# Which queue parks and fetches turned slabs, and where a short convolution stands in a projection, in a two-layer hybrid encoder

## The chip, the cores and the metric

One Trainium2 chip; the kernel uses one core. The metric is the device time of one execution in microseconds (us). Engines are named as in the profile: PE (TensorE), DVE (VectorE), ACT (ScalarE), POOL (GpSimd) and SP (SyncE, which only issues DMAs).

## The reference

Two layers of one block on x of 512 positions by 2048, with 256 memory tokens. Cut to what matters:

```python
for l in range(DEPTH):                       # DEPTH = 2
    h = rmsnorm(x, pre_norm_g[l])
    z = h @ w_in[l]                          # 2048 -> 4928 columns
    q_lat, kv_lat, k_pe, gb, gc, xin, q_mem, gate = split_cols(z)
    q = rmsnorm(q_lat, q_norm_g[l]) @ w_uq[l]            # 8 heads of 128 + 64, rotary on the 64
    kv = rmsnorm(kv_lat, kv_norm_g[l]) @ w_ukv[l]
    a_out = mla_attention(q, k, v)                       # k_pe, rotated, is shared by the heads
    u = gc * xin
    c_out = gb * conv3(u, conv_w[l])                     # width 3 over positions, 512 channels
    m_out = memory_attention(q_mem, rmsnorm(mem), w_mk[l], w_mv[l])
    y = concat([a_out, c_out, m_out]) * silu(gate)
    x = x + rmsnorm(y @ w_o[l], post_norm_g[l])
```

All is float32. The kernel makes each float32 product of three matmuls of a high and a low half.

## The kernel before

**Products.** The projection and the output projection use a Strassen-like scheme with seven products P1 to P7 in place of eight. The left operands (sums of quarters of h, each split in a high and a low half) lie in 14 slabs for the whole of a layer's projection: seven operands of two slabs each. A slab is a tile of 128 x 2048 float32; there are `SLABS = 19` of them (line 61), shared by everything that is large. The columns of `w_in` are taken in five groups: 0 (gc and xin), 1 (gb and part of the gate), 2 (the latents `lat` and the rotary key), 3 (part of the gate, gm, and the memory queries, qm), 4 (the rest of the gate, ga0 and ga1). Groups 2 to 4 use the passes `STEADY` (line 493): P1, then P5 and P2 in turn, then P6 and P3 in turn, then P7, then P4. Each product has four steps, one per block of weights, so a group has 28 steps: P1 is steps 0 to 3, P5/P2 4 to 11, P6/P3 12 to 19, P7 20 to 23, P4 24 to 27. A step is 12 matmuls.

**Weights.** A block of 128 x 1024 (512 KB) is loaded by SP into one of 8 `raw` buffers (line 157 through line 146). Some blocks are summed in place on DVE (L178: P5 and P6 add their block to that of P1). ACT casts the block to the high half `wh` (L189), DVE subtracts it to get the low half `wl` (L190); there are three buffers of each. P4 and P7 turn a block already there into another one by a DMA that adds (`more`, line 163, issued by POOL as soon as the `wl` that reads the old values is made): eight in a group, four for P4 and four for P7. In P6/P3 all eight `raw` buffers hold blocks that P7 and P4 still use.

**Passes end** in `ended` (line 551): the product's PSUM banks are read by ACT or DVE into the slabs of the group. P6, P7 and P4 go on adding into the banks of P1. In group 3 the end of P6 is the first write into the slab of qm; the matmuls of P7 that follow use the same banks.

**Parked slabs.** A result of the projection has positions on partitions; the mixer wants channels there. DVE transposes 32 x 32 blocks in place (L767, L1031, L1032), `sent` (line 938) writes the slab to DRAM by one DMA per part (L945), and `fetched` (line 948) reads it back into a slab in another order by four DMAs (L952). gb, gc, the latents ql and kvl (kvl in two parts), qm, gm, ga0 and ga1 go this way: 9 writes and 32 fetches in a layer. All of them are issued by SP, between its weight loads. After a fetch, `latents_parts` and `qm_parts` split the latents and qm in halves, and `conv` works.

**Convolution.** `conv_back` (line 967) fetches u (from gc) and y (from gb). `conv(l, c)` (line 971) does a quarter of the channels: two operations on ACT (L974, the copy that reads u, and L975), three on DVE (L976, L977, L979), in small tiles of which there are four. Its u slab is free when the fourth quarter has copied it.

**Order.** The source lists the steps of a group with other work between them (`put`, `add`; lines 1604 to 1661). For a step the program also prepares the blocks of the next two steps and issues loads up to eight blocks ahead. One line decides which engines keep that order:

```python
with tc.manual_schedule(engines={mybir.EngineType.PE, mybir.EngineType.SP, mybir.EngineType.Pool}):
    pr.run()
```

(line 1709). DVE and ACT are ordered when the kernel is built. Every engine, SP and POOL included, works through its own list in order, so an entry that waits holds up those behind it. The tile framework also decides at that time which free slab a new tile takes.

Other traffic that POOL issues in these stages: the memory keys and values (`mem_fetch`, L918), the rotary table (L1068), and in the mixer the rotated queries, written in two DMAs (L1107) and read back as QR in four (L1112) for each half of the heads.

Of the kernel before, what the change touches and what calls it, by code (L numbers as in the profile page):

```python
# [85 lines left out]
class Program:  # L86
# [23 lines left out]
    def add(self, fn, units=(), room=0.0, ahead=None):  # L110

        self.steps.append((list(units), fn, room, self.ahead if ahead is None else ahead))
# [115 lines left out]
def encoder(tc, x, xt, mem, memt, positions, columns, w_in, q_norm_g, w_uq, w_qr, kv_norm_g, w_ukv,  # L228
# [3 lines left out]
    nc = tc.nc  # L232
# [16 lines left out]
    add = pr.add  # L249

    G = {}
    n_id = [0]

    def nm(s):
        n_id[0] += 1
        return f"{s}_{n_id[0]}"
# [4 lines left out]
    def slab(name, dt=F32):  # L261
        return slabs.tile([P, D], dt, tag="slab", name=nm(name))

    def scrap(name, w=512, dt=F32):
        return piece.tile([P, 512], dt, tag="piece", name=nm(name))[:, :w]
# [657 lines left out]
    def spots(t, c=4):  # L923

        return t.rearrange("q (p c k) -> q c p k", p=4, c=c)

    def by_tokens(a):
        return a.rearrange("q (p k) -> q p k", p=4)
# [9 lines left out]
    def sent(key, *parts):  # L938

        n = sum(t.shape[-1] for t in parts) // 4  # L940
        d = G["sent", key] = dram.tile([4, P, n], F32, name=nm(f"sent{key}"))
        o = 0
        for t in parts:
            w = t.shape[-1] // 4
            nc.sync.dma_start(d[:, :, o:o + w].rearrange("b q k -> q b k"), t.rearrange("q (b k) -> q b k", b=4))  # L945
            o += w

    def fetched(key, name, c=4):

        t, d = slab(name), G.pop(("sent", key))  # L950
        for b in range(4):
            nc.sync.dma_start(t[32 * b:32 * b + 32, :512 * c].rearrange("i (p k) -> i p k", p=4),  # L952
                              d[b].rearrange("(p i) k -> i p k", p=4))
        return t

    def sent_rows(name, C):
        def f():
            pr.until(lambda: C.get((name, "turned")) == NT)
            sent(name, C[name, "slab"])
        return f  # L960

    def gate_back(k, name):
        def f():
            G["ys"][k] = spots(fetched(name, "y"))
        return f

    def conv_back():
        G["uw"] = fetched("gc", "u")
        G["ys"][2] = spots(fetched("gb", "y"))

    def conv(l, c):
        def f():
            u, y, w, g = scrap("u"), scrap("conv"), G[f"cw{l}"], G["ys"][2][:, c]
            nc.scalar.copy(by_tokens(u), spots(G["uw"])[:, c])  # L974
            nc.scalar.activation(y, u, AF.Copy, scale=w[:, 1, c:c + 1])  # L975
            nc.vector.scalar_tensor_tensor(y[:, 1:], u[:, :S - 1], w[:, 0, c:c + 1], y[:, 1:], op0=ALU.mult, op1=ALU.add)  # L976
            nc.vector.scalar_tensor_tensor(y[:, :S - 1], u[:, 1:], w[:, 2, c:c + 1], y[:, :S - 1],  # L977
                                           op0=ALU.mult, op1=ALU.add)
            nc.vector.tensor_tensor(g, by_tokens(y), g, op=ALU.mult)  # L979
        return f  # L980
# [32 lines left out]
    def latents_begin(l, C):  # L1013
        q, kv = G["ql"], G["kvl"] = slab("ql"), slab("kvl")
        tiles_of = lambda a: a.rearrange("p (g t j) -> p t g j", t=NT, j=32)
        normalise([v[:, :QR_] for v in C["lat"]], QR_, G["grow"][0], tiles_of(q), SC_MLA)
        normalise([v[:, O_KV:O_KV + KVR] for v in C["lat"]], KVR, G["grow"][1], tiles_of(kv[:, :1024]))

    def k_rope(l, C):
        m = scrap("kpm").rearrange("p (b t s i) -> p b t s i", b=2, t=NT, s=2)  # L1020
        m1, m2 = m[:, 0], m[:, 1]
        for t in range(NT):
            kp = C["lat"][t][:, O_PE:O_PE + ROPE].rearrange("p (s i) -> p s i", s=2)
            nc.vector.tensor_tensor(m1[:, t], kp, G["cos2"][:, t], op=ALU.mult)
            for s in range(2):
                nc.vector.tensor_tensor(m2[:, t, s, :], kp[:, 1 - s, :], G["sin2"][:, t, s, :], op=ALU.mult)
        kr = G["kvl"][:, 1024:1536].rearrange("p (g t j) -> p t g j", t=NT, j=32)
        nc.vector.tensor_tensor(kr[:, :, :2], m1, m2, op=ALU.add)
        nc.scalar.copy(kr[:, :, 2:], kr[:, :, :2])
        for h in (slice(0, 1024), slice(1024, D)):  # L1030
            pr.defer(1.2, lambda h=h: nc.vector.transpose(G["ql"][:, h], G["ql"][:, h]))  # L1031
        pr.defer(1.8, lambda: nc.vector.transpose(G["kvl"][:, :1536], G["kvl"][:, :1536]))  # L1032
        pr.defer(0.0, lambda: G.update(normalised=l))

    def latents_sent(l):
        pr.until(lambda: G.get("normalised") == l)
        sent("ql", G.pop("ql"))
        kv = G.pop("kvl")
        sent("kvl", kv[:, :1024], kv[:, 1024:1536])
# [429 lines left out]
    def put(*passes):  # L1469
        for steps in passes:  # L1470
            for s in steps:
                add(*s)
# [20 lines left out]
    for l in range(depth):  # L1493
        G["left"] = L = Left(l > 0)
        C, gs, owns = projection(l)
# [44 lines left out]
        else:  # L1540
            put(ms[:1])
            add(use)
            for n in range(8):
                t, h = n // 2, n % 2
# [60 lines left out]
        steps = [s for passes in gs[2] for s in passes]  # L1605
# [9 lines left out]
        steps = [s for passes in gs[3] for s in passes]  # L1615
        put(steps[:2])
        add(lambda l=l, C=C: latents_begin(l, C))
        put(steps[2:5])
        add(conv_back)
        put(steps[5:8])  # L1620
        add(lambda l=l, C=C: k_rope(l, C))
        put(steps[8:18])
        add(lambda l=l: pr.until(lambda: G.get("normalised") == l))
        put(steps[18:20])
        add(conv(l, 0))
        put(steps[20:22])
        add(conv(l, 1))
        put(steps[22:23])
        add(lambda l=l: latents_sent(l))
        put(steps[23:24])  # L1630
        add(conv(l, 2))
        put(steps[24:26])
        add(conv(l, 3))
        put(steps[26:])
        add(owns[4])
        g4 = [s for steps in gs[4] for s in steps]
        put(g4[:3])
        add(latents_back)
        put(g4[3:6])
        add(sent_rows("qm", C))  # L1640
        if l == 0:
            add(tables_wide)
        put(g4[6:8])
        add(sent_rows("gm", C))
        put(g4[8:9])
        add(latents_parts)
        put(g4[9:11])
        add(lambda: G.update(qmw=fetched("qm", "QmL")))
        put(g4[11:14])
        if l == 0:  # L1650
            add(tables_turned)
        put(g4[14:20])
        add(qm_parts)
        put(g4[20:23])
        add(gate_back(3, "gm"))
# [97 lines left out]
```

## Time and profile before

| | |
|---|---|
| median of 3 runs | 1486.68 us (1485.53 to 1490.99) |
| the profiled execution | 1484.13 us, span 1482.3 us |
| granted TensorE clock, mean | 0.987 |
| PE busy | 98% of the span |
| DVE, ACT, POOL busy | 77%, 59%, 16% |
| DMA | 309.60 MB, 209 GB/s in the mean |
| weight loads of w_in by SP, 512 KB each | median 5.8 us to landing |

A line of a group of instructions reads: source line, engine, operation, the tile written and the tiles read, shape, count, then busy time and mean nanoseconds of one, then idle time of the engine just before them and what ended it. A line of waits reads: who waited, for whom, total us, times, longest. In a timeline the columns are start, duration (us), engine, line, operation; brackets hold the idle time before it. SPq and POOLq stand for a queue's DMA issues. In the time before, groups 3 and 4 of the first layer lie between about 271 and 435 us, of the second between about 1006 and 1170 us.

### The profile page before, as it was taken

The numbers are of one execution on the slowest core, as the hardware profiler recorded it, in microseconds if no ns is written. First come the engines' busy times: TensorE is split into PE (matmuls) and PEld (weight loads), VectorE is DVE, ScalarE is ACT, GpSimd is POOL, SyncE is SP. The second block draws the span as 40 slices with busy tenths as digits, with TensorE's granted clock in tenths as the row PEclk, the third lists the DMA queues.
The fourth block names the chain that finished last, engine by engine and source line by source line (L and its number), as shares of the span: only waits on it lengthen the run. The fifth ranks groups of instructions, "written<-read, shape, count | busy, mean of one in ns | idle before, by whom it ended". The sixth has DMA issues, their size and how long they took to land.

```text
span 1482.3 us, 19184 instructions
## 1 busy us (share of the span) xinstructions
PE 1445.9 (98%) x6944; PEld 1227.9 (83%) x6944; DVE 1140.0 (77%) x1517; ACT 869.6 (59%) x1330; POOL 239.7 (16%) x248
## 2 busy tenths in 40 slices
PE   9999999989899999999999999999898999999997
PEld 8888889868788888888898888998687888888886
DVE  5899688877667778868879666768766777688687
ACT  7856344644557788654777434445444586776543
POOL 0031302120111010321210333021201110003101
PEclk9999999989999999999999999999899999999999
DMA  9999959688899293795987999596888993228983
GB/s 358 404 271 212 222 157 234 177 174 251 214 276 253 69 270 93 134 224 155 336 288 226 239 229 218 186 209 169 174 249 208 292 242 90 53 86 147 258 177 128
DMA packets 155039, 309.60 MB, mean 209 GB/s; under 512 B 11009, under 2 KB 35073, under 8 KB 151105
## 3 DMA queue, kind: packets, MB, share of 16 engines
q1 hardware_dynamic: 105472, 194.86, 42.8%
q0 software_dynamic: 49472, 113.52, 37.1%
q8 instruction: 54, 0.88, 0.3%
q14 instruction: 41, 0.33, 0.1%
HBM read 270.47 MB, written 37.88 MB: 208 GB/s over the span
## 4 chain that ended last, share of the span: by engine, by line
PE 75%; issue 9%; DVE 6%; DMA 5%; POOL 2%; ACT 2%; POOLq 0%; SPq 0%; DVEq 0%; ACTq 0%
PE P L273 17%; PE P L274 17%; PE P L272 17%; DMA wr<-in_w_in_dram 3%; PE ptp L1219 2%; DVE wl L190 2%; POOL wr L146 2%; PE o L273 1%; PE o L274 1%; PE o L272 1%; PE sc L274 1%; PE sc L273 1%; PE sc L272 1%; PE sc L1200 1%; PE qps L274 1%
## 5 line engine op out<-in xcount | busy, mean ns | idle before, releaser
L189 ACT CAST wh<-wr 128x1024 fp32r<-128x1024 f32 (+2 forms) x436 | 443.6, 1023 | 442.3 <-PE P L274 311.1
L190 DVE TENSOR_TENSOR wl<-wr,wh 128x1024 fp32r<-128x1024 f32 (+2 forms) x436 | 513.6, 1184 | 219.9 <-ACT wh L189 216.9
L272 PE MATMUL P<-wh,S 128*128 128x512 f32 (+1 forms) x896 | 346.6, 387 | 12.5 <-ACT wh L189 12.5
L273 PE MATMUL P<-wl,S 128*128 128x512 f32 (+1 forms) x896 | 346.7, 387 | 3.7 <-DVE wl L190 3.7
L274 PE MATMUL P<-wh,S 128*128 128x512 f32 (+1 forms) x896 | 345.3, 385 | 0.0
L272 PE MATMUL P<-wh,A 128*128 128x512 f32 (+1 forms) x656 | 254.5, 388 | 6.2 <-ACT wh L189 6.2
L273 PE MATMUL P<-wl,A 128*128 128x512 f32 (+1 forms) x656 | 254.1, 387 | 2.4 <-DVE wl L190 2.4
L274 PE MATMUL P<-wh,A 128*128 128x512 f32 (+1 forms) x656 | 253.3, 386 | 0.0
L146 POOL DMA_DIRECT2D wr<-in_w_in_dram x108 | 130.3, 1212 | 503.3 <-DVE wl L190 399.5
L272 PEld LDWEIGHTS P<-wh,S 128*128 128x128 f32 x896 | 169.8, 189 | 44.1 <-ACT wh L189 13.3
L273 PEld LDWEIGHTS P<-wl,S 128*128 128x128 f32 x896 | 169.5, 189 | 36.5 <-DVE wl L190 6.0
L274 PEld LDWEIGHTS P<-wh,S 128*128 128x128 f32 x896 | 169.6, 189 | 30.5
L272 PEld LDWEIGHTS P<-wh,A 128*128 128x128 f32 x656 | 124.1, 189 | 29.2 <-ACT wh L189 7.0
L273 PEld LDWEIGHTS P<-wl,A 128*128 128x128 f32 x656 | 124.2, 189 | 26.3 <-DVE wl L190 4.4
L274 PEld LDWEIGHTS P<-wh,A 128*128 128x128 f32 x656 | 124.3, 189 | 22.4
L146 POOL DMA_DIRECT2D wr<-in_w_o_dram x40 | 48.5, 1286 | 299.0 <-DVE wl L190 293.3
L1206 ACT ACTIVATE P<-sc,nm 128x512 f32<-128x512 f32 (+1 forms) x96 | 59.7, 622 | 27.1 <-DVE nm L1203 26.9
L178 DVE TENSOR_TENSOR wr<-wr,wr 128x1024 f32<-128x1024 f32 (+1 forms) x60 | 69.6, 1164 | 7.1 <-DMA wr<-in_w_in_dram 6.5
L1209 ACT ACTIVATE P<-P,rec 128x512 f32<-128x512 f32 (+1 forms) x96 | 62.4, 661 | 7.5 <-DVE rec L1208 7.5
L1203 DVE TENSOR_REDUCE nm<-sc 128x1 f32<-128x512 f32 (+1 forms) x96 | 56.7, 594 | 10.4 <-PE sc L1201 9.3
L1219 PE MATMUL ptp<-identr,P 128*128 128x128 f32 x320 | 46.1, 272 | 0.3 <-ACT P L1209 0.3
L1219 PEld LDWEIGHTS ptp<-identr,P 128*128 128x128 f32 x320 | 38.2, 140 | 6.5 <-ACT P L1209 0.7
(311 smaller groups left out, 2053.4 us busy)
## 6 DMA issues: line engine op xcount, KB each, us to landing
wr<-in_w_in_dram SPq DMA_DIRECT2D x128, 512.0 KB, 5.8
wr<-in_w_in_dram POOLq DMA_DIRECT2D x92, 512.0 KB, 7.8
wr<-in_w_o_dram SPq DMA_DIRECT2D x48, 512.0 KB, 6.3
wr<-in_w_o_dram POOLq DMA_DIRECT2D x40, 512.0 KB, 6.7
wr<-in_w_in_dram SPq DMA_DIRECT2D x32, 416.0 KB, 4.1
wr<-in_w_mk_dram SPq DMA_DIRECT2D x15, 512.0 KB, 8.6
wr<-in_w_mv_dram SPq DMA_DIRECT2D x15, 512.0 KB, 9.9
wr<-in_w_in_dram POOLq DMA_DIRECT2D x16, 416.0 KB, 6.6
```

Source lines behind the costliest of these rows:

```text
L146: engine.dma_start(dst, src, **kw)
L178: nc.vector.tensor_tensor(tiles[a], tiles[a], tiles[b], op=ALU.add)
L189: pin(nc.scalar.copy(hi[:, h], src[:, h]))
L190: pin(nc.vector.tensor_tensor(lo[:, h], src[:, h], hi[:, h].bitcast(F32), op=ALU.subtract))
L272: nc.tensor.matmul(ps, ah, bh, start=first, stop=False, **kw)
L273: nc.tensor.matmul(ps, ah, bl, start=False, stop=False, **kw)
L274: nc.tensor.matmul(ps, al, bh, start=False, stop=last, **kw)
L1200: nc.tensor.matmul(by_tokens(ps), q, G["KA"], start=False, stop=False)
L1203: nc.vector.tensor_reduce(nmax, ps, axis=AX.X, op=ALU.max, negate=True)
L1206: nc.scalar.activation(pt, ps, AF.Exp, bias=nmax, accum_out=tot)
L1209: nc.scalar.activation(pt, pt, AF.Copy, scale=rec)
L1219: nc.tensor.transpose(ps[:, k * P:(k + 1) * P], pt[:, k * P:(k + 1) * P], G["ident"])
```

## The change

The DMAs of `sent` and `fetched` are issued by GpSimd instead of SyncE. In group 3, the fetch of u and y moves from behind step 4 to behind step 2; the four quarters of the convolution move from behind steps 19, 21, 23 and 25 of group 3 to behind steps 21 and 24 of group 3 and steps 0 and 2 of group 4; the write of the latents moves from behind step 22 to behind step 20. In group 4, the fetch of the latents moves from behind step 2 to behind step 1, the writes of qm and gm from behind steps 5 and 7 to behind steps 4 and 5, the latents' split from behind step 8 to behind step 6, and the fetch of qm from behind step 10 to behind step 9. In the first layer the rotary table's transposes move from behind step 13 to behind step 8. Steps are counted from 0 here.

```diff
         for t in parts:
             w = t.shape[-1] // 4
-            nc.sync.dma_start(d[:, :, o:o + w].rearrange("b q k -> q b k"), t.rearrange("q (b k) -> q b k", b=4))
+            nc.gpsimd.dma_start(d[:, :, o:o + w].rearrange("b q k -> q b k"), t.rearrange("q (b k) -> q b k", b=4))
             o += w
...
         for b in range(4):
-            nc.sync.dma_start(t[32 * b:32 * b + 32, :512 * c].rearrange("i (p k) -> i p k", p=4),
+            nc.gpsimd.dma_start(t[32 * b:32 * b + 32, :512 * c].rearrange("i (p k) -> i p k", p=4),
                               d[b].rearrange("(p i) k -> i p k", p=4))
...
-        put(steps[2:5])
+        put(steps[2:3])
         add(conv_back)
-        put(steps[5:8])
+        put(steps[3:8])
         add(lambda l=l, C=C: k_rope(l, C))
         put(steps[8:18])
         add(lambda l=l: pr.until(lambda: G.get("normalised") == l))
-        put(steps[18:20])
+        put(steps[18:21])
+        add(lambda l=l: latents_sent(l))
+        put(steps[21:22])
         add(conv(l, 0))
-        put(steps[20:22])
+        put(steps[22:25])
         add(conv(l, 1))
-        put(steps[22:23])
-        add(lambda l=l: latents_sent(l))
-        put(steps[23:24])
-        add(conv(l, 2))
-        put(steps[24:26])
-        add(conv(l, 3))
-        put(steps[26:])
+        put(steps[25:])
         add(owns[4])
         g4 = [s for steps in gs[4] for s in steps]
-        put(g4[:3])
+        put(g4[:1])
+        add(conv(l, 2))
+        put(g4[1:2])
         add(latents_back)
-        put(g4[3:6])
+        put(g4[2:3])
+        add(conv(l, 3))
+        put(g4[3:5])
         add(sent_rows("qm", C))
+        put(g4[5:6])
+        add(sent_rows("gm", C))
         if l == 0:
             add(tables_wide)
-        put(g4[6:8])
-        add(sent_rows("gm", C))
-        put(g4[8:9])
+        put(g4[6:7])
         add(latents_parts)
-        put(g4[9:11])
-        add(lambda: G.update(qmw=fetched("qm", "QmL")))
-        put(g4[11:14])
+        put(g4[7:9])
         if l == 0:
             add(tables_turned)
-        put(g4[14:20])
+        put(g4[9:10])
+        add(lambda: G.update(qmw=fetched("qm", "QmL")))
+        put(g4[10:20])
         add(qm_parts)
```

## The prediction, made before the result was known

> **What bounds the kernel now.** I read the page first, then who TensorE (PE) waits for, then the stretches in which it waits, and last the queues of the engines that release it.
>
> ```profile
> PE 1445.9 (98%) x6944; PEld 1227.9 (83%) x6944; DVE 1140.0 (77%) x1517; ACT 869.6 (59%) x1330; POOL 239.7 (16%) x248
> ```
>
> ```profile
> PE P L272 <- ACT wh L189: 18.6, 4, 6.2
> PE P L273 <- DVE wl L190: 6.1, 9, 1.0
> ```
>
> PE is the bound: whatever does not open or close a gap in PE costs nothing. Of its waits four carry nearly all, each for a weight block's high half `wh` (18.6 us), then for the low half `wl` of the same block. By window they lie in groups 3 and 4 of the projection, one in each, in both layers:
>
> ```profile
> 309.40:322.30 12.90, 5.66 (x13) 3.99 (x13) 12.10 (x15) 5.00 (x6) 3.66 (x3) 0.60 0.40 66
> 387.60:397.20 9.60, 5.78 (x14) 4.06 (x13) 6.30 (x7) 5.61 (x7) 0.00 (x0) 0.65 0.39 98
> 1045.20:1059.50 14.30, 7.05 (x17) 5.01 (x16) 12.13 (x14) 5.89 (x7) 3.67 (x3) 0.64 0.44 73
> 1124.10:1134.55 10.45, 6.39 (x16) 4.62 (x15) 7.15 (x8) 5.62 (x7) 0.82 (x1) 0.67 0.44 105
> ```
>
> Columns: stretch, length, then busy time and (instructions) of PE, weight load, DVE, ACT, POOL, granted clock, DMA share, GB/s. I set the edges where even pace ends and returns. The pace is in PE's timeline, at the start of group 3 and at the first gap:
>
> ```profile
> 270.71 0.39 PE L272 MATMUL P<-wh,A 128*128 128x512 f32 x1
> ...
> 271.39 0.39 PE L272 MATMUL P<-wh,A 128*128 128x512 f32 x1
> ```
>
> ```profile
> 309.20 0.39 PE L274 MATMUL P<-wh,S 128*128 128x512 f32 x1
> 315.83 0.79 PE L272 MATMUL P<-wh,S 128*128 128x512 f32 x1 [6.24 <-ACT wh L189]
> ```
>
> Three matmuls in 0.68 us is one each 0.227 us, a step of 12 in 2.72 us, a group of 28 steps in 76.2 us; 309.20 ends step 13 (counted from 0), and step 14 waits. The windows hold 12, 12, 15 and 14 matmuls of their own (the x counts less one or two tails from before the edge), worth 2.7, 2.7, 3.4 and 3.2 us. So the gaps cost 12.9-2.7 = 10.2, 9.6-2.7 = 6.9, 14.3-3.4 = 10.9 and 10.45-3.2 = 7.3 us: **35.3 us** in all. That is more than the 24.7 us of waiting, because the granted clock is only 0.60 to 0.67 there.
>
> Why does the first gap come? DVE and ACT:
>
> ```profile
> 310.16 0.75 DVE L976 SCALAR_TENSOR_TENSOR conv<-u,cols,conv 128x511 f32<-128x511 f32 x1 [0.85 <-ACT conv L975]
> ...
> 313.42 1.22 DVE L178 TENSOR_TENSOR wr<-wr,wr 128x1024 f32<-128x1024 f32 x1
> ...
> 321.56 0.42 DVE L386 COPY widecos<-cos 128x512 f32<-128x512 f32 x1
> ```
>
> ```profile
> 386.52 0.59 ACT L578 COPY ga<-P 128x512 f32<-128x512 f32 x1 [5.62 <-PE P L274]
> 387.88 0.58 ACT L578 COPY ga<-P 128x512 f32<-128x512 f32 x1 [0.77 <-PE P L274]
> 388.36 1.05 ACT L277 CAST ckv<-ckvL 128x1024 fp32r<-128x1024 f32 x1
> 389.31 0.62 ACT L277 CAST ckvL<-ckvL 128x512 fp32r<-128x512 f32 x1
> 389.83 1.04 ACT L189 CAST wh<-wr 128x1024 fp32r<-128x1024 f32 x1
> ```
>
> The sum that step 14 needs (L178 at 313.42) stands in DVE's queue behind conv work whose source lines come six to twelve steps later; even `tables_wide` (L386, from group 4) ran at 321.56. So DVE and ACT do not follow the source: line 1709 fixes only PE, SP and POOL, and the build orders DVE and ACT by when it believes inputs arrive. The second gap is order alone: ACT idles 5.62 us, copies a finished pass out, splits `ckv`, and only then (389.83) casts the block PE wants. Why would the build believe weights are late? SP's queue:
>
> ```profile
> 289.74 1.89 SPq L952 DMA_DIRECT2D u<-sentgc  x4
> 291.68 3.01 SPq L952 DMA_DIRECT2D y<-sentgb  x4
> 295.71 0.39 SPq L146 DMA_DIRECT2D wr<-in_w_in_dram  x1
> ```
>
> ```profile
> 368.09 1.47 SPq L146 DMA_DIRECT2D wr<-in_w_in_dram  x2
> ```
>
> ```profile
> DMA to landing us min/median/max: 9.5/9.7/10.2
> ```
>
> ```profile
> DMA to landing us min/median/max: 8.2/8.3/8.5
> ```
>
> ```profile
> wr<-in_w_in_dram SPq DMA_DIRECT2D x128, 512.0 KB, 5.8
> ```
>
> Right ahead of both gaps eight slab fetches stand in front of weight loads, and those (three issued 295 to 300, two 368 to 370) take 9.7 and 8.3 us to land against a median of 5.8. The pair of 368.09 had landed by 377.7, long before 389.83: in the second gap the data were there and only the order was wrong.
>
> **The change part by part.** *SP loses 9 writes and 32 fetches a layer.* Its weight loads no longer queue behind slabs, in the chip or in the build's timeline. I therefore let the build put sums and casts ahead of conv and latent splits, and take the 35.3 us off. The bounds are 0 (order unchanged) and 35.3; I stand near the upper end, since all four gaps follow the same eight fetches and no other stretch with a weight stream has such a gap.
>
> The Trainium skill (DMA: Bandwidth & Descriptors, SWDGE vs HWDGE vs iDMA) says each DMA engine takes turns between hardware and software queues. By that rule weights would share the engines with the moved slabs rather than stand behind them; no row here has slabs on POOL beside weights on SP, and the sum does not use it.
>
> *POOL gains them.*
>
> ```profile
> L1112 POOL DMA_DIRECT2D QR<-qrd x16 | 8.8, 555 | 11.1 <-PE sc L274 4.9 <-DMA qrd<-qrh 3.5 <-DMA qrd<-rm 2.1
> L146 POOL DMA_DIRECT2D wr<-in_w_in_dram x108 | 130.3, 1212 | 503.3 <-DVE wl L190 399.5 <-DMA wr<-in_w_in_dram 68.0 <-issue 21.5
> ```
>
> ```profile
> DMA to landing us min/median/max: 5.9/10.0/13.5
> ```
>
> ```profile
> sentql<-ql SPq DMA_DIRECT2D x2, 1024.0 KB, 6.3
> ```
>
> ```profile
> 301.51 1.27 POOL L146 DMA_DIRECT2D wr<-in_w_in_dram  x1 [23.06 <-DVE wl L190]
> ```
>
> The third row is QR's. A slab fetch has its size and costs POOL 0.56 us. For a write (twice the rows of a 1.2 us weight accumulate) I bound 0.56 to 2.4 and take 1.2, nearest in kind. Per layer 32 x 0.56 + 9 x 1.2 = 29 us (23 to 40): POOL goes from 240 to about 298 us, 20% busy, nothing on the path. Landing, 10.0 us for that size, stays under the lead of the fetches. What is queued behind them on POOL: the fetch of u and y, behind step 2 of group 3, stands after the two `pow` of the latents and ahead of eight weight accumulates (L146), the first at 301.5; even if it leaves as late as SP's did (289.7), it is issued by 294.2, 7 us before. The latents' writes stand behind all eight. The qm fetch, now behind step 9 of group 4, stands ahead of that group's accumulates; the first of these is used at step 20, ten steps or 27 us later. I cost all of this at 0, hidden under those 7 and 27 us; with that cover gone PE waits in P7 or P4, microsecond for microsecond. In the mixer the ga writes now precede the QR traffic on POOL:
>
> ```profile
> PE sc L1200 <- DMA QR<-qrd: 0.2, 1, 0.2
> ```
>
> QR has no spare time in one layer. The writes leave earlier than from SP, and the ga fetches then follow QR instead of running beside it; I cost 0, with up to 2.4 x 2 = 5 us a layer lost or 0.2 gained.
>
> The Trainium skill (SBUF — State Buffer, Who interferes with whom) speaks against the change: GpSimd cannot write descriptors while DVE runs in a two-port mode, so such DMAs belong on SP. If every DVE operation here counted, each of the 41 issues a layer could wait for one of about 1.2 us, 49 us more of POOL and still off the path; the 1212 ns above, with DVE 77% busy, show no such stretch for this mix.
>
> *Conv.*
>
> ```profile
> L976 DVE SCALAR_TENSOR_TENSOR conv<-u,cols,conv 128x511 f32<-128x511 f32 x4 | 3.0, 740 | 0.8 <-ACT conv L975 0.8
> L977 DVE SCALAR_TENSOR_TENSOR conv<-u,cols,conv 128x511 f32<-128x511 f32 x4 | 3.0, 738 | 0.1
> L979 DVE TENSOR_TENSOR y<-conv,y 128x512 f32<-128x512 f32 x4 | 2.6, 685 | 0.0
> ```
>
> 8.6 us of DVE in group 3; two quarters move on, 4.3 us, if the build follows (it hoists freely, so perhaps not). DVE stays crowded there, and I leave 2 us a layer of small PE waits (0 to 4.3). Group 4 gets as much and has idle DVE time in the 6.9 us gap: 0.
>
> The sum: -35.3 + 2 x 2 = -31.3 us. The profiled execution took 1484.1 (span 1482.3 and 1.8 around it), so 1452.8; it lies 2.6 us under the median of the runs, 1486.7, and the forecast for the median is **1455.4**. With the QR and DVE bounds this case reaches from 1451 to 1470.
>
> **The rivals.** *A slab comes free too late.* In group 3 fourteen of the 19 slabs hold left operands; gm, ql, kvl, u and y fill the rest. Before, conv's last copy of u ran in the first gap, ahead of that eviction, and qm could take u's place. Now conv 2 and 3 stand in group 4, and unless the build hoists their copies, qm's first eviction waits until ql is written out, behind POOL's last accumulate:
>
> ```profile
> 330.81 1.20 POOL L146 DMA_DIRECT2D wr<-in_w_in_dram  x1 [1.51 <-DVE wl L190]
> ```
>
> That is 8.5 us after step 15 began (322.3); plus 1.2, plus 6.3 landing, qm is evicted 16.0 us after it, while P7 needs the bank after 5 steps, 13.6 us. PE waits 2.4 us plus two evictions of 0.7 (the size of L979's), and at 2.4 us per write and slower landing up to 8, with the clock loss: about 7 a layer, 1455.4 + 14 = **1469**. Against it: ACT is idle enough to copy u early.
>
> *The order stays.* The build may still see late weights, or hoist conv because its data come earlier. Then gaps move but remain: **1487**, within 7. For it: conv was hoisted up to twelve steps.
>
> *ACT and DVE wait for POOL's slabs (slower).* If the build believes fetches land sooner than they do, a split or conv copy stands at the head of an engine's queue while its slab is in flight, and casts behind it starve PE. Lead is about two steps, 5.4 us; QR's slowest fetch took 13.5 us, and before the change there is this:
>
> ```profile
> ACT wh L189 <- DMA ckvL<-sentkvl: 1.7, 1, 1.7
> ```
> An event costs 13.5-5.4 = 8 plus 2 of clock, 10 us; there are eight (u/y, latents, qm, gates in two layers). From four events on the 35.3 is eaten; with five, 1486.7-35.3+50 = **1501**. Against it: before, that one wait of 1.7 us is all. The Trainium skill's two-port rule, above (SBUF — State Buffer, Who interferes with whom), would make such lateness likelier.
>
> **How the numbers follow.** Forecast 0.57, late slab 0.20, order stays 0.11, slower 0.12. The range 1449 to 1480 takes the first two with their bounds, 2 us below for the spread of the runs, and the milder part of the third (one gap of four gone). Half a per cent, 7.4 us, is about what a measurement can tell from none: faster 0.78, same 0.10, slower 0.12.
>
> **What would show it.** Right: weight loads of groups 3 and 4 land in about 5 us; PE's waits for `wh` L189 fall from 18.6 to under 4; the granted clock is 1.0 from step 10 of group 3 through group 4; SP has no L945 or L952. The slab rival: PE waits at step 20 of group 3, released by DVE's eviction into qm. The order rival: conv or ckv still ahead of a sum or cast. The slower one: ACT or DVE idle, ended by a DMA out of a sent tensor. I am wrong if PE's gaps keep their 35 us, or new ones exceed 10.

## The result

The kernel after the change takes 1474.83 us (median of 7 runs, 1469.56 to 1477.41) against 1485.28 us (7 runs, 1482.27 to 1490.99) for the kernel before: the ratio is 0.9924, 95% interval 0.9901 to 0.9946, or 10.45 us less. The forecast was 31.3 less. The profiled execution of after took 1476.04 us (span 1474.3). One execution of e12, a kernel tried below, took 2935 us, with matmuls every 0.44 us from first to last where the others have 0.227 and no record of the granted clock in its trace; it stands in no comparison.

Busy times first, then what PE waited for, from the page and from the waits of PE (us in all, times, longest):

```profile
PE 1442.1 (98%) x6944; PEld 1223.7 (83%) x6944; DVE 1138.1 (77%) x1517; ACT 868.7 (59%) x1330; POOL 288.6 (20%) x330
```

```profile
PE P L273 <- DVE wl L190: 19.8, 13, 5.7
PE P L272 <- ACT wh L189: 1.9, 1, 1.9
```

POOL went from 239.7 to 288.6 us. PE's waits for `wh` fell from 18.6 to 1.9 us, and those for `wl` rose from 6.1 to 19.8. One kind of wait has taken the place of another.

Where does the time come from and go to? I took the start of each PE matmul in both traces, matched by their order and tiles, and read how far after leads or lags at fixed places of before. The table gives by how much that lag grew in each stretch (us of the profiled executions, negative is a gain). Columns are stretches of before: layer 0's group 2 and the start of group 3 (220 to 300), the first old gap (300 to 345), the first steps of group 4 (345 to 383), the second old gap (383 to 400), the rest of group 4 (400 to 450); then layer 1's first old gap (1020 to 1065), first steps of group 4 (1065 to 1120) and second old gap (1120 to 1145). What the columns leave out comes to under 4 us, but for e12_again, as told there.

| kernel | g2 | gap 1 | g4 first | gap 2 | g4 rest | layer 1: gap 1 | g4 first | gap 2 |
|---|---|---|---|---|---|---|---|---|
| after | +5.9 | -10.3 | +6.7 | -6.9 | +5.8 | -11.6 | +8.0 | -7.3 |
| e1 queue alone | +2.4 | -8.6 | +5.9 | -6.9 | +2.9 | -7.7 | +8.3 | -7.3 |
| e2 steps alone | -0.1 | -2.8 | +0.9 | -1.5 | -1.0 | -3.1 | +0.3 | -6.0 |
| e3 qm first | +4.1 | -10.3 | +8.0 | -6.0 | -1.7 | -11.2 | +9.2 | -7.3 |
| e4 sums held | +4.2 | -10.3 | +0.9 | -6.9 | +0.3 | -11.2 | 0.0 | -6.6 |
| e5 before, conv held | +0.7 | +4.0 | 0.0 | -1.5 | -0.3 | -10.8 | +14.1 | -1.0 |
| e9 queue alone, sums held | +5.6 | -8.3 | 0.0 | -6.9 | +0.9 | -8.1 | 0.0 | -7.3 |
| e10 steps alone, sums held | +0.9 | -4.1 | +0.9 | +0.7 | -0.6 | -4.0 | +0.6 | +4.6 |
| e11 sums and conv held | +6.2 | +2.9 | +0.9 | -5.3 | +0.3 | -11.6 | +12.4 | -3.7 |
| e12_again | +2.8 | -10.3 | 0.0 | -6.0 | +9.7 | -11.2 | +2.6 | -6.8 |

The four old gaps are gone, all of them: 10.3 + 6.9 + 11.6 + 7.3 = 36.1 us against 35.3 in the sum. But 5.9 + 6.7 + 5.8 + 8.0 = 26.4 us came back elsewhere. The windows show it, with the columns of the prediction's windows (granted clock, DMA share and GB/s last):

```profile
300.00:320.00 20.00, 20.00 (x89) 16.28 (x88) 19.74 (x21) 13.16 (x18) 4.93 (x4) 1.00 0.73 160
...
350.00:364.00 14.00, 10.72 (x48) 8.57 (x47) 7.16 (x7) 7.07 (x9) 0.29 (x1) 1.00 1.02 313
...
387.00:400.00 13.00, 9.53 (x43) 7.55 (x41) 4.01 (x4) 3.18 (x4) 4.08 (x7) 0.96 0.89 201
...
1082.00:1096.00 14.00, 9.79 (x43) 7.79 (x42) 6.38 (x7) 6.96 (x9) 0.19 (x1) 0.97 1.01 296
```

Where group 3 stood still for 10 us PE is now busy throughout at full clock. The holes are now in group 4. Here is the first, in the timelines of PE, DVE, ACT and POOL:

```profile
359.50 0.39 PE L272 MATMUL P<-wh,A 128*128 128x512 f32 x1
363.17 0.50 PE L273 MATMUL P<-wl,A 128*128 128x512 f32 x1 [3.28 <-DVE wl L190]
```

```profile
352.63 1.23 DVE L190 TENSOR_TENSOR wl<-wr,wh 128x1024 fp32r<-128x1024 f32 x1 [0.23 <-ACT wh L189]
360.16 1.22 DVE L178 TENSOR_TENSOR wr<-wr,wr 128x1024 f32<-128x1024 f32 x1 [6.31 <-DMA wr<-in_w_in_dram]
361.30 0.70 DVE L767 STREAM_TRANSPOSE gm<-gm 128x512 f32<-128x512 f32 x1
361.93 1.18 DVE L190 TENSOR_TENSOR wl<-wr,wh 128x1024 fp32r<-128x1024 f32 x1
```

```profile
354.74 1.05 ACT L189 CAST wh<-wr 128x1024 fp32r<-128x1024 f32 x1
```

```profile
341.18 2.20 POOL L952 DMA_DIRECT2D cqL<-sentql  x4 [3.00 <-DMA sentql<-ql]
344.76 2.18 POOL L952 DMA_DIRECT2D ckvL<-sentkvl  x4 [1.38 <-DMA sentkvl<-kvl]
349.53 0.76 POOL L945 DMA_DIRECT2D sentqm<-qm  x1 [2.58 <-DMA cqL<-sentql]
```

DVE alternates one `wl` for each cast of ACT, so the `wl` of 361.93 belongs to the cast of 354.74, which ended at 355.8. It could have run then, 6 us sooner. But in DVE's queue a sum (L178) stands ahead of it, and that sum waits 6.31 us for its weight load. The prediction had before's illness as sums *behind* other work; now a sum is *too far ahead*. DVE's whole waiting of this kind, from the waits of the two kernels, before and then after:

```profile
DVE wr L178 <- DMA wr<-in_w_in_dram: 6.5, 7, 1.5
```

```profile
DVE wr L178 <- DMA wr<-in_w_in_dram: 43.8, 23, 8.8
```

The load is late while the slabs move beside it. SP's weight loads of these first steps, issue to landing, before (345 to 358 us) and after (340 to 353 us):

```profile
DMA to landing us min/median/max: 3.8/4.5/7.4
```

```profile
DMA to landing us min/median/max: 9.6/12.6/14.3
```

The rows of 350 to 364 us show what differs: before moved 204 GB/s at a DMA share of 0.70, after moves 313 at 1.02. Before met its burst of slabs some 21 us later, and there two loads right behind the eight fetches on SP's own queue took 8.2 to 8.5 us (the prediction's rows). Loads that meet the burst from the other queue were later than that, not earlier.

```profile
350.00:364.00 14.00, 14.00 (x63) 11.59 (x63) 11.28 (x11) 7.91 (x10) 0.00 (x0) 1.00 0.70 204
```

The Trainium skill (DMA: Bandwidth & Descriptors, SWDGE vs HWDGE vs iDMA) has each DMA engine take turns between the software and the hardware queue, and the trace is in line with it: the loads were neither stopped nor untouched by the burst, they took 12.6 us in place of 4.5. The prediction named this rule and kept it out of its sum.

### The profile page after: what moved, and what is told of

The parts are those of the page before. It is cut to its first block, busy times and chain, and to the rows that moved or that the text cites. A ratio compares the mean times of both kernels' runs of the same rounds, so it can differ in the third digit from the quotient of the medians.

```text
span 1474.3 us, 19214 instructions
## 1 busy us (share of the span) xinstructions
PE 1442.1 (98%) x6944; PEld 1223.7 (83%) x6944; DVE 1138.1 (77%) x1517; ACT 868.7 (59%) x1330; POOL 288.6 (20%) x330
## 4 chain that ended last, share of the span: by engine, by line
PE 71%; DMA 10%; DVE 8%; issue 8%; ACT 2%; POOL 1%; POOLq 0%; SPq 0%; DVEq 0%; ACTq 0%
PE P L273 16%; PE P L274 16%; PE P L272 15%; DMA wr<-in_w_in_dram 7%; DVE wl L190 4%; PE ptp L1219 2%; PE o L273 1%; PE o L274 1%; PE o L272 1%; PE sc L274 1%; PE sc L273 1%; PE sc L272 1%; ACT wh L189 1%; PE qps L272 1%; POOL wr L146 1%
## 5 line engine op out<-in xcount | busy, mean ns | idle before, releaser
L273 PE MATMUL P<-wl,A 128*128 128x512 f32 (+1 forms) x656 | 253.9, 387 | 10.3 <-DVE wl L190 10.3
L178 DVE TENSOR_TENSOR wr<-wr,wr 128x1024 f32<-128x1024 f32 (+1 forms) x60 | 70.0, 1168 | 44.4 <-DMA wr<-in_w_in_dram 43.8
```

Of the source, the lines that this page charges most:

```text
L178: nc.vector.tensor_tensor(tiles[a], tiles[a], tiles[b], op=ALU.add)
L273: nc.tensor.matmul(ps, ah, bl, start=False, stop=False, **kw)
```

## The experiments

Theories. *Order*: the loss in group 4 is a matter of where the build puts sums on DVE. *Lateness*: it is the burst of slabs that makes loads late. And for the gain: *queue* against *placement* of the steps. In kernels with added lines the line numbers shown here are up to 5 higher than in after.

**Each half of the change alone.** e1 is the kernel before with `nc.gpsimd` for `nc.sync` in `sent` and `fetched`; e2 is the kernel after with `nc.sync` there.

> The kernel before with only the queue changed: the slab writes and fetches (L945, L952) go from SP to POOL, every step stays where it was. Queue theory (the gain comes from the build reordering DVE and ACT once SP's weight loads no longer stand behind slabs): the gaps of groups 3 (10.2 and 10.9 us) are gone without any conv being moved, so at least 18 of the 21 us; the loss of about 6 us in group 2 of layer 0 (237 and 262 us) is there too, since nothing else could cause it; and the slab traffic is spread over a longer stretch than in the kernel after, so the gaps of group 4 are smaller than its 20 us: 1458 to 1470 us. Placement theory (the conv spread over two groups is what freed DVE in group 3): the group 3 gaps stay, 1478 to 1486 us.

> The kernel after with the slabs back on SP, every moved step where the change put it. Queue theory: the four gaps of before come back in about their old places, group 2 of layer 0 has no gap, 1478 to 1490 us. Placement theory: the group 3 gaps stay away, 1462 to 1472 us.

e1 took 1477.05 us (ratio 0.9940, 0.9923 to 0.9957), e2 1473.01 (0.9911, 0.9885 to 0.9937). The waits of PE in e1 and in e2:

```profile
PE P L273 <- DVE wl L190: 16.7, 14, 4.2
PE P L272 <- ACT wh L189: 1.9, 3, 0.9
```

```profile
PE P L272 <- ACT wh L189: 9.0, 3, 3.3
PE P L273 <- DVE wl L190: 8.2, 12, 1.5
```

The queue alone removes nearly all of the old gaps (30.5 of 36.1 us), with no conv moved, and brings the same new waits for `wl` as after. My expected time was too low, since group 4 loses 17.1 us here too (20.5 in after); group 2 lost 2.4 us where I expected about 6. For e2 both theories were wrong. The queue theory expected no gain, and the placement theory expected group 3 free of gaps: the old gaps are still there but shorter (22.7 of their 36.1 us are left, the longest wait is 3.3 us for 6.2), and nothing is lost in group 4. The two halves don't add: alone they are worth 8.7 and 12.7 us, together 10.5.

**Hold the sums.** e4 is after with each sum of group 4 kept behind the DVE instruction traced just before it:

```
-  nc.vector.tensor_tensor(tiles[a], tiles[a], tiles[b], op=ALU.add)
+  total = nc.vector.tensor_tensor(tiles[a], tiles[a], tiles[b], op=ALU.add)
+  if self.tight:          # set from the last conv of group 3 to the end of group 4
+      self.pin(total)     # tc.keep_in_program_order
```

> The kernel after with each sum L178 of group 4 held behind the DVE instruction traced just before it, so that the build can't put it ahead of a wl that is already castable. DMA traffic is the same. Order theory (a sum waits at the head of DVE's queue for its load and the ready wl stands behind it): the loads still land 11 to 15 us after issue, but the gaps at 359.5 and 1090.7 shrink from 3.4 and 4.4 to under 1 us and the stall at 396 from 5.9 to under 3; 1456 to 1463 us. Bandwidth theory (the 16 DMA engines are full at 300 GB/s from 320 to 364 us and PE runs out of weights whatever stands where): the gaps only move a step on and keep their sum, 1472 to 1477 us.

1457.38 us, ratio 0.9811 (0.9786 to 0.9836): 17 us faster than after. Waits of PE, landing of SP's loads from 340 to 353 us, DVE's timeline and the window:

```profile
PE P L276 <- DVE wl L193: 6.5, 11, 1.1
PE P L275 <- ACT wh L192: 1.5, 2, 0.9
```

```profile
DMA to landing us min/median/max: 12.9/13.1/13.7
```

```profile
354.31 1.22 DVE L193 TENSOR_TENSOR wl<-wr,wh 128x1024 fp32r<-128x1024 f32 x1 [0.93 <-ACT wh L192]
...
356.55 1.23 DVE L193 TENSOR_TENSOR wl<-wr,wh 128x1024 fp32r<-128x1024 f32 x1 [0.39 <-ACT wh L192]
357.69 1.22 DVE L179 TENSOR_TENSOR wr<-wr,wr 128x1024 f32<-128x1024 f32 x1
```

```profile
350.00:364.00 14.00, 14.00 (x63) 11.58 (x63) 9.94 (x10) 9.76 (x13) 0.76 (x1) 1.00 0.97 325
```

The loads are as late as in after, the DMA engines as full, and PE loses nothing in this stretch. The sum comes two `wl` later and finds its load landed; in the whole kernel DVE's sums wait 8.6 us for loads, in after 43.8. So bandwidth as such does not bind in these steps; a late load hurts through the sum that waits for it ahead of ready work.

**The stall at 396 us.** In after PE also stops for 5.73 us from 396 us on, waiting for a `wl`. There the fetch of qm leaves POOL at 387.8 us, behind the writes of the rotary table. e3 is after with two lines of layer 0 exchanged:

```
-        if l == 0:
-            add(tables_turned)
         put(g4[9:10])
         add(lambda: G.update(qmw=fetched("qm", "QmL")))
+        if l == 0:
+            add(tables_turned)
```

> The kernel after with the fetch of qm put ahead of tables_turned in layer 0 (in layer 1 nothing changes). If the stall at 396 us comes from the qm fetch standing behind the table transfer on POOL, so that it leaves at 387.8 beside the weight load and the accumulate that PE wants next, it now leaves near 370 and the stall is gone: 5.9 us and about 1 of clock, 1467 to 1470 us, layer 1 unchanged. If that weight block is late for another reason (its buffer came free late), the stall stays within 2 us and the time within 3 of 1474.8.

1468.7 us (0.9889, 0.9867 to 0.9912). The rest of group 4 goes from +5.8 to -1.7 us; the first steps still lose 8.0 and, in layer 1, 9.2. The time lies in the range expected.

**Both together, and group 2.** e6 is e4 with e3's exchange and the sums of group 2 held too.

> The kernel after with the sums of groups 2 and 4 held behind what is traced before them, and qm fetched ahead of tables_turned. Order theory: what is left of the losses after the sums of group 4 were held (1457.4 us: about 4 us in group 2 of layer 0, 3 us late in group 4) goes in part, 1450 to 1456 us. If group 2's loss is a matter of late loads and not of order, it stays at 1457.

1458.76 us (0.9819, 0.9793 to 0.9845): no better than e4, and above the 1450 to 1456 us of the order theory. By PE's starts, group 2's loss fell from 4.2 to 1.9 us, and e3's gain was not to be had twice, since with the sums held no stall was left at 396. Group 2 of layer 0 lost 1.9 to 6.2 us in every kernel with slabs on POOL and under 1 in those with slabs on SP. The rest of its cause stays open.

**Is the queue needed, once the order is right?** e5 is the kernel before with conv and the latents' splits held back; e8 adds the held sums of group 4.

```
-            nc.scalar.copy(by_tokens(u), spots(G["uw"])[:, c])
+            hold(nc.scalar.copy(by_tokens(u), spots(G["uw"])[:, c]))   # tc.keep_in_program_order
...          # likewise the first conv operation on DVE, and the casts of cq, ckv
```

> The kernel before, slabs on SP and every step where it was; only the conv operations and the splits of the latents are held behind what is traced before them on DVE and ACT, so that the build can't put them ahead of sums and casts. DMA queues and issue places are untouched. Order theory (the gaps of before are an order, and the queue mattered only because it changed the order that the build chose): the gaps at 309 and 1045 go (21 us), those at 387 and 1124 shrink as far as the splits of ckv no longer stand ahead of the cast; 1453 to 1466 us, without any slab moved. Queue theory of the prediction (weights are really late behind eight slab fetches, 8 to 10 us): PE still waits for loads after the slabs, 1470 to 1484 us.

> The kernel before with conv and the latents' splits held as in the last kernel but two, and the sums of group 4 held as well; slabs on SP throughout. If the queue itself is worth nothing once the order is good, this comes to the time of the kernel after with its sums held, 1457 us, within 5 us either way. If slabs on SP cost PE something that order can't hide, it stays above 1465 us.

Both are slower than before: 1492.63 us (1.0051, 1.0034 to 1.0069) and 1497.08 (1.0075, 1.0050 to 1.0100). Neither of e5's ranges holds its time, and e8 is 40 us above e4. The old gap at 309 us did go (a wait of 0.42 us is left), with loads after the slabs as late as in before, 8.7 to 9.9 us. But another gap came 16 us later. PE's waits in e5:

```profile
PE P L272 <- DVE qm L551: 23.7, 2, 12.0
```

That is the prediction's first rival: with conv in the order of the source, u keeps its slab, and qm's first eviction must wait until ql is written out (DVE's evictions of qm wait 17.3 us for that write in the two layers). So before's order was not merely bad: hoisting conv cost 10 us a layer and saved a wait of 12, or 14 with the clock.

**The rival in the kernel after.** e11 is e4 with conv and the splits held as in e5.

> The kernel e4 (after, sums of group 4 held) with the conv operations and the splits of the latents held as well, so that conv's copies of u run where the source has them and u's slab stays taken into group 4. Slab theory (the prediction's first rival; seen on SP as a wait of 12 us a layer for qm's first eviction): qm waits until ql is written out, on POOL behind the last accumulate, and PE stops some 8 to 14 us in each layer at the 20th step of group 3, 1475 to 1490 us. If on POOL the write of ql leaves early enough, or another slab is free, no such wait: within 4 us of 1457.

1486.10 us (1.0002, 0.9988 to 1.0017), 29 more than e4. Timelines of DVE and PE:

```profile
341.15 1.28 DVE L554 TENSOR_TENSOR qm<-gm,P 128x512 f32<-128x512 f32 x2 [9.78 <-DMA sentql<-ql]
```

```profile
331.36 0.39 PE L277 MATMUL P<-wh,S 128*128 128x512 f32 x1
341.99 0.77 PE L275 MATMUL P<-wh,S 128*128 128x512 f32 x1 [10.24 <-DVE qm L554]
```

PE waits 10.2 us a layer for the slab, 12 to 13 with the clock. In after the rival was absent for the reason that the prediction gave against it, an ACT with time to copy u early. ACT's timeline there has the last of the four copies of u 10 us before qm's first eviction, at 330.5:

```profile
320.90 0.62 ACT L974 COPY u<-u 128x512 f32<-128x512 f32 x1
```

**Each half with the sums held.** e9 is e1, e10 is e2, each with e4's edit.

> Only the queue changed (POOL), every step where it was in the kernel before, and the sums of group 4 held as in e4. If the moved steps (conv over two groups, earlier fetches) are worth nothing once the order is good, this comes to the time of e4, 1457 us, within 4. If conv's move frees DVE in group 3 as the change has it, small gaps there keep it above 1463.

> Only the steps moved, slabs on SP, and the sums of group 4 held as in e4. Moving the steps alone left gaps of 3.4 us (about 5 with the clock) in group 3 of both layers, released by a cast that waits for a sum behind conv work; those sums are not held, so they stay, and group 4 had lost little: 1468 to 1474 us. If the queue is worth nothing once group 4's order is held, 1457.

e9 takes 1461.28 us (0.9840, 0.9805 to 0.9875): 4 us behind e4, within their spread (1457.18 to 1467.07 and 1454.37 to 1460.80), so the moved steps are worth little once the order is good. e10 takes 1486.36 (1.0010, 0.9993 to 1.0028): 29 us behind, and 13 slower than without the held sums, which I had not expected. By the table its four old gaps keep 6.2, 7.6, 7.2 and 11.2 us that e4 does not have. PE's four waits there:

```profile
307.15 0.50 PE L275 MATMUL P<-wh,A 128*128 128x512 f32 x1 [2.89 <-ACT wh L192]
...
389.53 0.80 PE L275 MATMUL P<-wh,S 128*128 128x512 f32 x1 [4.72 <-ACT wh L192]
...
1038.63 0.49 PE L275 MATMUL P<-wh,A 128*128 128x512 f32 x1 [2.96 <-ACT wh L192]
...
1124.53 0.80 PE L275 MATMUL P<-wh,S 128*128 128x512 f32 x1 [7.31 <-ACT wh L192]
```

The two in group 3 are those of e2 (3.27 and 3.30 us): the cast stands behind conv work, which nothing holds. At 389.53 the cast waits for a sum that stands behind the latents' splits. The last is of another kind. ACT and then the write of qm, in e10; the write of qm in e4:

```profile
1119.88 1.04 ACT L280 CAST ckv<-ckvL 128x1024 fp32r<-128x1024 f32 x1 [5.87 <-DMA sentqm<-qm]
1123.43 1.99 ACT L192 CAST wh<-wr 128x1024 fp32r<-128x1024 f32 x2 [2.50 <-DVE wr L179]
```

```profile
L948 SPq DMA_DIRECT2D sentqm<-qm x2: 366/366/367, 376.8 to 1109.7; - x2
```

```profile
L948 POOL DMA_DIRECT2D sentqm<-qm x2: 761/761/761, 347.4 to 1069.8; - x2
```

The split of ckv stands at the head of ACT's queue until qm is written out, and the casts that PE wants stand behind it. This happens in layer 1 alone; in layer 0 the split runs at 384.5 us, before qm is written out. On SP that write goes out at 1109.7, on POOL at 1069.8 (layer 0: 376.8 and 347.4); with the lag between the two kernels taken off (16.2 and 4.0 us, as in the table), qm leaves some 24 us sooner on POOL. So with the sums of group 4 held the queue is still worth 29 us in these two kernels. About 11 of them go with a slab that leaves early; the other three gaps are again an order on ACT and DVE that the queue changes.

**Is lateness needed too?** e7 is after with its slab traffic spread (ckv fetched behind step 6 of group 4, qm and gm written behind 9, qm fetched behind 14). e12 adds the fetches of the latents one by one:

```
+        for b in range(2, 8):
+            put(g4[b + 1:b + 2])
+            add(latents_back(b))     # block b of cq, then of ckv
...
+        put(g4[11:15])
         add(lambda: G.update(qmw=fetched("qm", "QmL")))
```

> The kernel after with the slab traffic of group 4 spread: cq is fetched where it was, the fetch of ckv comes behind step 6, qm and gm are written behind step 9, qm is fetched behind step 14. The build leaves the sums as far ahead on DVE as in the kernel after. If both are needed, a sum at the head of the queue and a load that is late since the DMA engines are full, then the loads issued there land in 6 to 9 us in place of 12 to 15, the gaps at 359.5 and 1090.7 go though the order is the same, and the time falls by 5 to 15 us, 1460 to 1470 (the stall near 396 may stay, at another place). If the order alone makes the gaps, whatever the landing, the time stays within 3 us of 1474.8.

> The kernel after with the eight fetches of the latents issued one a step (steps 2 to 9 of group 4), qm written behind step 10 and gm behind 11, qm fetched behind 15; the build leaves the hoisted sums where the kernel after has them. If late landing is needed for the loss in group 4, as well as the order, the loads issued between 341 and 352 us land in 4 to 8 us, the sum waits under 2 us, the gaps at 359.5 and 1090.7 are under 1 us, and the time falls to 1460 to 1468. If the order alone does it, or if the same bytes only make the same lateness later, gaps of 3 to 6 us remain in group 4 of each layer and the time stays within 4 of 1474.8.

> The same kernel once more (latents fetched one a step), for a profile: its one profiled execution ran at half PE pace throughout and shows no waits. The other six took 1471 to 1476 us, as long as the kernel after. Order theory: PE's gaps of group 4 are still there, each behind a sum that waits at the head of DVE's queue, though the loads issued between 341 and 352 us land sooner than the 12 to 15 us of the kernel after; the gaps of group 4 add to 6 us or more a layer with the clock. Lateness theory: those gaps are gone and the time was lost elsewhere.

> The kernel with the latents fetched one a step, and the sums of group 4 held as in e4. Order theory: holding the sums takes off the same 17 us whether the loads are late or not, 1455 to 1461 us. If pacing adds to it (loads on time let PE run where e4 still lost 3 us late in group 4), 1450 to 1455. If pacing had moved the loss into group 3 or the mixer, it stays above 1465.

By time e7 and e12 are where order alone would have them: e7 1476.12 us (0.9930, 0.9906 to 0.9955), e12 1471.46 to 1476.44 in six runs (0.9926, 0.9908 to 0.9944), e12_again 1472.63 (2 runs). e13, which is e12 with the sums held, took 1470.53 (0.9898, 0.9862 to 0.9933), not the 1455 to 1461 that the order theory expected. The profiles say more. In e7 the gap at the old place is gone, where the sum waits 2.47 us, but three steps further on, beside ckv's fetch at its new place, both come together again. DVE and PE in e7:

```profile
366.87 1.23 DVE L178 TENSOR_TENSOR wr<-wr,wr 128x1024 f32<-128x1024 f32 x1 [5.67 <-DMA wr<-in_w_in_dram]
```

```profile
369.29 0.50 PE L273 MATMUL P<-wl,A 128*128 128x512 f32 x1 [3.32 <-DVE wl L190]
```

Then e12_again. Its fetches did not come one a step, since POOL keeps only its own order and nothing stood between them, but ckv's left 19 us behind cq's. Landing of SP's loads from 339 to 350 us, DVE's timeline, and ACT's some 50 us on:

```profile
DMA to landing us min/median/max: 5.8/8.5/11.2
```

```profile
351.77 1.23 DVE L178 TENSOR_TENSOR wr<-wr,wr 128x1024 f32<-128x1024 f32 x1 [1.65 <-DMA wr<-in_w_in_dram]
352.91 0.70 DVE L767 STREAM_TRANSPOSE gm<-gm 128x512 f32<-128x512 f32 x1
353.54 1.18 DVE L190 TENSOR_TENSOR wl<-wr,wh 128x1024 fp32r<-128x1024 f32 x1
```

```profile
409.54 2.01 ACT L988 ACTIVATE QmH<-QmL 128x1024 fp32r<-128x1024 f32 x2 [2.25 <-DMA QmL<-sentqm]
...
420.42 2.94 ACT L189 CAST wh<-wr 128x1024 fp32r<-128x1024 f32 x3 [6.34 <-DMA wr<-in_w_in_dram]
```

DVE has the same order as in after, the sum ahead of the `wl`. But its load is 1.65 us late, not 6.31, and PE has no gap in the first steps of either layer at that place (0.0 in the table, +2.6 in layer 1 from a gap six steps further on). So in the first steps the loss of after needs both: a sum out in front and a load that is late. Break either and it is gone. The time did not fall: 9.7 us went in the rest of group 4, and 7.2 more at the same place of layer 1, behind the table's last column. There the qm fetch, moved to step 15, stands beside the accumulates of the blocks behind it, which take 10.7 to 14.4 us to land (6.0 to 8.3 in after, for those of 402 to 412 us), and its own split waits for it on ACT. No run moves that fetch alone, so this cause is read, not tried. Holding the sums takes little of that away (e13: 7.8 and 7.4), since no sum is in it.

## Why the prediction was wrong

Point by point, in its own steps.

- *The four gaps, 35.3 us*: right. 36.1 us went.
- *Why they would go*: half right. With the queue change alone DVE and ACT run in another order and 30.5 of the 36.1 us go (e1). But "I stand near the upper end" rested on the eight fetches that delay weight loads. Shorter gaps with the slabs still on SP (e2) show that the moved steps alone take part of them away, and e5 that the loads of before, as late as they were, did not stop PE at 309 us.
- *DVE crowding in group 3, 2 us a layer*: not seen; the window of 300 to 320 us has PE full.
- *POOL, 298 us, fetches at 0.56*: right, 288.6; a write took 0.75 to 0.84, not 1.2, and only the fetches of gm took more than forecast (1.06 us in the median).
- *"I cost all of this at 0, hidden under those 7 and 27 us"* and *"Group 4 gets as much and has idle DVE time ...: 0"*: **the step that failed.** Both ask only whether POOL and DVE have time. Neither asks what 2.75 MB of latents and qm, sent off within 9 us of each other with nothing ahead of them, do to the loads on the other queue, nor whether the build's new order puts a sum that needs such a load ahead of ready work. The first steps of group 4 lose 6.7 and 8.0 us that way. The qm fetch, whose cost was put at 0 too, left beside a load and an accumulate that PE wanted next, 5.8 us more. That is 20.5 us in group 4 where the sum has 0. Held sums get back 17 (e4).
- *Group 2 of layer 0*: not in the prediction; 5.9 us, its cause in part open.
- *What it would be wrong by*: "or new ones exceed 10" is what came. Weight loads of group 3 did land in 4.3 us (median, 285 to 300 us), those of group 4 in 12.6.
- *The rivals.* The order did not stay: all four gaps went. The late slab did not come, and e11 shows it at 12 to 13 us a layer, not 7, once conv is held. The slower rival had the right form, an engine whose queue head waits on a transfer, and the wrong transfer: the longest wait of ACT or DVE for a slab in after is 1.7 us (`ckvL`); it was a weight load beside them. The Trainium skill (PSUM — Partial Sum Buffer, Engine vs sequencer instructions) has DVE's queue strictly in order; the ready `wl` of 361.93 behind the waiting sum agrees.

The forecast of 1455.4 us is within 2 us of e4, which is the change and one more edit: the gain was there, and most of its price was paid one stage further on. That the two times are so close is partly luck: group 2's 4.2 us, which nobody forecast, stand in e4 where the sum had 4 us for crowding that did not come.

## What to carry to other kernels

Where the build chooses the order of an engine's queue, moving transfers to another queue changes two things at once: how late loads really are, and the order that the build chooses. (That it goes by modelled arrivals is the prediction's reading; the runs show only that the order changed.) After such a move look for instructions that wait at the head of an in-order queue with ready work behind them, and try holding those back; here one pin was worth 17 us, more than the change itself. It is no rule: with the slabs on SP the same pin made the kernel 13 us slower (e10 against e2), and holding conv back cost 29 (e11 against e4). What stands early may be what sets a buffer free. Cost a moved transfer by its bytes in the stretch where it lands, beside what already moves there, and by the buffer that it sets free, not by the issuing engine's spare time.

## What the runs showed of the hardware

- Weight loads on SP's queue took 12.6 us (median) beside a burst of slabs on POOL's queue, at 313 GB/s and a DMA share of 1.02, and 4.5 us at 0.70 and 204 GB/s.
- Two loads right behind eight slab fetches on SP's own queue took 8.2 to 8.5 us (before, 368 us).
- On POOL a slab fetch took 0.55 to 0.59 us in the median of each slab, with DVE 77% busy; only those of gm had a median of 1.06. A write took 0.75 to 0.84.
